# Layer change of a two-layer transformer kernel: last output round by token groups, norm factors through a diagonal, context modulated early, one modulation job on TensorE

## The chip, the cores and the metric

The kernel runs on one core of one Trainium2 chip. The metric is device time in microseconds (us), from the first to the last instruction of the program, as the median of several runs. The engines of a core run their own instruction streams in order and meet at semaphores: PE is TensorE (matmuls), DVE is VectorE, ACT is ScalarE, POOL is GpSimd, and SP issues the transfers here.

## The reference

Two layers act on 512 latent tokens and 256 context tokens of width 2048. In each layer the stream is normalised, modulated, projected, passed through four groups of attention heads with a gate, projected back, normalised, gated and added:

```python
for l in range(DEPTH):
    with_ctx = l < DEPTH - 1
    shift, scale, gate = jnp.split(silu_c @ w_mod[l] + b_mod[l], 3, axis=-1)
    shift_c, scale_c, gate_c = jnp.split(silu_cc @ w_mod[l] + b_mod[l], 3, axis=-1)
    n = rms_norm(h, pre_norm_g[l]) * (1.0 + scale[:, None]) + shift[:, None]
    nc = rms_norm(hc, pre_norm_g[l]) * (1.0 + scale_c) + shift_c
    p = jnp.split(n @ w_in[l], split_points, axis=-1)
    pc = jnp.split(nc @ w_in[l], split_points, axis=-1)
    ...
    y = (jnp.concatenate([oa, ob, on, od], axis=-1) * jax.nn.silu(p[12])) @ w_out[l]
    h = h + gate[:, None] * rms_norm(y, post_norm_g[l])
    if with_ctx:
        yc = (jnp.concatenate([oa_c, ob_c, on_c, od_c], axis=-1) * jax.nn.silu(pc[12])) @ w_out[l]
        hc = hc + gate_c * rms_norm(yc, post_norm_g[l])
return h
```

Everything is fp32. The next layer needs rms_norm(h), so its norm factor (one number for each token) is known only when all 2048 columns of a token's h are.

## The kernel before

Weights and activations are split into a high and a low part, and every fp32 product is three matmuls on the parts (`mm3`, L301 to L303; `split`, L292 on ACT for the high part, L293 on DVE for the low one). Weight tiles stream in as `wr`, become `wh` and `wl`, and stand in a pool; activations stand split in a large tile called `arena`.

A layer begins with the input projection. Its first column blocks are computed in pairs by seven products of sums of operands in place of eight (`START` and `ORDER` give the order of the products; for the first pair of a layer 1, 2, 6, 5, 7, 3, 4). A product is a *slot* of 8 k steps. The operands are token halves: `token_half` transposes one k of one half of the tokens on PE (L557), applies scale and shift on ACT (L559: one activation for latent tokens from PSUM, one for context tokens that it has loaded), and `reloads` splits the operands into the arena. `token_sums` forms sums of them for the later products. `token_n` (transposes at L548) does the other eight k later, within layer 1's stream.

A layer ends with `out_phase`. The output projection runs in rounds: one round is one block of 512 columns for four tiles of 128 latent tokens, 16 k by 12 matmuls. `evac` takes a round's result from PSUM (L1414 ACT with the sum of squares, L1415 DVE with the gate). After the last round `tail` forms the root (`rstd_of`, a chain of 9 or so small DVE instructions, L514 to L531), adds the residual (L1437, DVE; POOL at L1435 in places for the last layer), squares h on ACT for the next norm (L1443), forms the second root and scales h by it (L1452 ACT, L1454 DVE, the tile is `z`). The last round holds back its last `gs` k: it does them for tiles 0 and 1 first, then for 2 and 3, so that the first two tiles' evacuation runs beside the others' matmuls; gs is 2 in layer 0, 4 in layer 1.

While layer 0's rounds run, the next layer's modulation vectors are computed as side steps: each `mod_steps` job streams a block of `w_mod` through three `mraw` buffers and accumulates it on DVE (L441, L443), folds the halves, and sums over partitions on PE (L474). Queue orders follow the order in which the program writes its steps and a scheduler's placement of the side steps among the slots (`drive`). Layer 1's first weight tiles are prepared in the same stretch (L166 to L179, L293).

Of the kernel before, what the change touches and what calls it, by code (L numbers as in the profile page):

```python
# [47 lines left out]
RAWS = 6  # L48

# [33 lines left out]
class Kernel:  # L83
# [104 lines left out]
    def split_one(self, kind, g, key):  # L188
        if not self.need(g, 0):
            return False  # L190
        raw = g[0]
        if kind == "og":
            l, s, k = key
            hi, lo = self.og[s, k] = self.og_tiles(s, k)
        else:
            hi, lo = self.new_pair()
        self.split(hi, lo, raw)
        self.retire(g, 0)
        return True

    def load_one(self):
        nc, a = self.nc, self.a
        if self.live >= self.raws or self.wload >= len(self.lq):
            return False
        g, i, (kind, key) = self.lq[self.wload]
        if kind == "og" and key not in self.stored:
            return False
        raw = self.wp.tile([P, 512], F32, tag="wr", bufs=RAWS, name="wr")
        if kind == "in":
            l, b, c = key  # L210
            nc.sync.dma_start(raw, a["w_in"][l, b, :, 4 * c:4 * c + 4, :].rearrange("p k c -> p (k c)"))
        elif kind == "out":
            l, k, c = key
            nc.sync.dma_start(raw, a["w_out"][l, k * P:(k + 1) * P, c * 512:(c + 1) * 512])
        else:
            l, s, k = key
            w0, w = ((0, SEQ), (SEQ, CTX))[s]
            raw = raw[:, 0:w]
            nc.sync.dma_start(raw, self.ogd[l, k, :, w0:w0 + w])
        g[i] = raw  # L220
        self.live += 1
        self.wload += 1
        return True
# [81 lines left out]
    def run(self):  # L305
        tc, nc, a = self.tc, self.nc, self.a
        with ExitStack() as es:
# [41 lines left out]
            self.cnd = self.dp.tile([KT, P, CTX], F32, name="cnd")  # L349
            self.arena = base.tile([P, 7 * 8 * HT], F32R, name="arena")  # L350
# [6 lines left out]
    def plan(self):  # L357
# [8 lines left out]
        for l in range(DEPTH):  # L366
# [7 lines left out]
            for s in ((1, 0) if l < DEPTH - 1 else (0,)):  # L374
                for r in range(2 if s else 4):
                    for k in self.order:
                        if r == 0 and k != self.order[-1]:
                            self.push_one("og", (l, s, k))
                        for c in ((2 * r, 2 * r + 1) if s else (r,)):
                            self.push_one("out", (l, k, c))  # L380
# [161 lines left out]

    def token_n(self, l, k, tiles, n, t):
# [3 lines left out]
        for i, ht in enumerate(tiles):  # L547
            nc.tensor.transpose(t[:, i * P:(i + 1) * P], ht[:, k * P:(k + 1) * P], self.ident)  # L548
# [3 lines left out]
    def token_half(self, l, k, tiles, h, n, t):  # L552

        nc = self.nc
        nc.sync.dma_start(n[:, 2 * P:HT], self.cnd[k, :, h * P:(h + 1) * P])
        for i in range(2):
            nc.tensor.transpose(t[:, i * P:(i + 1) * P], tiles[2 * h + i][:, k * P:(k + 1) * P], self.ident)  # L557
        for s, view, src in ((0, n[:, 0:2 * P], t[:, 0:2 * P]), (1, n[:, 2 * P:HT], n[:, 2 * P:HT])):
            nc.scalar.activation(view, src, AF.Identity, scale=self.mA[:, l, s, k:k + 1], bias=self.mB[:, l, s, k:k + 1])  # L559
# [152 lines left out]

    def next_layer(self, l, tiles, tail):

        op = self.op


        rows = [op.tile([P, D], F32, tag="h", bufs=4, name="n") for _ in range(2)]
        ns = [[rows[k // 5][:, k % 5 * HT:(k % 5 + 1) * HT]] for k in range(8)]
        first = [lambda k=k: self.token_half(l, k, tiles, 0, ns[k][0], self.bank(1 + k % 2)) for k in range(8)]  # L720
        for a, b in zip_longest(tail, [None] * 8 + first):
# [3 lines left out]
        more = [op.tile([P, D], F32, tag="h", bufs=4, name="n") for _ in range(2)]  # L725
        for k in range(8):
            ns[k].append(more[k // 5][:, k % 5 * HT:(k % 5 + 1) * HT])
        ts = [t[:, o * HT:(o + 1) * HT] for t in (rows[1], more[1]) for o in (3, 4)]
        ts += [op.tile([P, 512], F32, tag="gp", bufs=3, name="tt")[:, 0:HT] for _ in range(3)]
        ts.append(op.tile([P, HT], F32, tag="tt", name="tt"))  # L730
        ts = [ts[2 * j:2 * j + 2] for j in range(4)]
# [4 lines left out]
        self.first = self.reloads(ns, ts)  # L736
        self.ns2 = []

        def begin():
            t = [op.tile([P, D], F32, tag="h", bufs=4, name="n") for _ in range(4)]  # L740
# [610 lines left out]
    def out_phase(self, l):  # L1351
# [3 lines left out]
        gs = 4 if last else 2  # L1355
# [3 lines left out]
        def round_slots(s, ntok, cs, done=None, early=False):  # L1359
# [18 lines left out]
            def finish(c, n0, done):  # L1378
# [3 lines left out]
                for tiles in ((0, 1), (2, 3)):  # L1382
# [8 lines left out]
            slots = [lambda n=n, c=c: slot(n, c) for n in range(KT if done is None else KT - gs) for c in cs]  # L1391
            if done is not None:
                slots.append(lambda: finish(cs[0], KT - gs, done))
# [23 lines left out]
        def tail(s, tiles, bufs, xeng):  # L1417
# [37 lines left out]

            steps = [start] + [lambda i=i, c=c: resid(i, c) for i in tiles for c in range(4)]
            if not last:
# [16 lines left out]
        if not last:  # L1474
# [6 lines left out]
            mods = self.mod_steps([(l + 1, k, c, (0, 1)) for c in range(3) for k in (1, 0)])  # L1481
# [6 lines left out]
        def xeng(i, c):  # L1488
            return nc.scalar if i % 2 else nc.vector

        for r in rounds:
            def done(tiles):
                evac(tiles, (3,), *state["acc"], state["bufs"])
                todo = tail(0, tiles, state["bufs"], xeng)
# [31 lines left out]
        self.next_layer(l + 1, state["bufs"][0], steps)  # L1526
# [81 lines left out]
```

## Time and profile before

| | us |
|---|---|
| median of 3 runs | 2696.28 (2694.01 to 2699.97) |
| profiled execution | 2691.34, its span 2689.5 |
| PE busy / DVE busy / ACT busy | 2583.6 / 2136.9 / 1285.6 |
| layer change, end of the last round to the first pair of blocks done | 1516.7 to 1583.3 |
| PE busy in it | 32.2 of 66.6 |
| last matmul of the program, last add, end of span | 2671.3, 2685.05, 2689.5 |

Times in rows of a profile are microseconds from the start of the span. A row of the timeline has the start, the duration, the engine, the line of the kernel, the tiles written and read, and in brackets how long the engine had stood idle and what released it. A row with xN groups N instructions that follow one another. A row of windows has busy time of PE, its weight loads, DVE, ACT and POOL, each with its number of instructions, then the granted clock of PE, the share of the DMA engines, and GB/s.

### The profile page before, as it was taken

What the parts mean: (1) busy time and instruction counts of PE and PEld (TensorE: products, weight loads), DVE (VectorE), ACT (ScalarE), POOL (GpSimd) and SP (SyncE); (2) the same over time, 40 slices, a digit from 0 to 9 for tenths busy, and PEclk for the clock granted to TensorE, in tenths of its full rate; (3) what the DMA queues carried; (4) which work ended last, traced back from release to release, by engine and by line L of the source; (5) the groups of instructions that cost most, each with busy time, mean ns of one, the idle gap of its engine ahead of it and who ended that gap; (6) DMA issues with size and microseconds to landing.
All of it is one profiled execution on the core that took longest, in us unless ns stands there. A gap on an engine that the chain in (4) does not pass through costs nothing. (4 is left out here: it accounts for less than half of the span.)

```text
span 2689.5 us, 41459 instructions
## 1 busy us (share of the span) xinstructions
PE 2583.6 (96%) x14392; PEld 2230.1 (83%) x14392; DVE 2136.9 (79%) x4408; ACT 1285.6 (48%) x2532; POOL 44.1 (2%) x42
## 2 busy tenths in 40 slices
PE   7899999999999999999999689999999999999997
PEld 1699999988888888887777479999978888888885
DVE  3899998678889888766889989787688887776524
ACT  3534343455556455546533464444455554544422
POOL 0000000000000000000010000000000000000001
PEclk9999999999999999999999889999999999999998
DMA  9455554422333444426886535443533434453622
GB/s 310 146 193 193 196 191 157 159 91 88 96 112 120 132 134 148 142 89 220 299 274 217 204 129 172 144 148 136 170 97 95 131 126 152 154 162 122 226 98 98
DMA packets 240994, 421.59 MB, mean 157 GB/s; under 512 B 27360, under 2 KB 68624, under 8 KB 240272
## 3 DMA queue, kind: packets, MB, share of 16 engines
q1 hardware_dynamic: 230288, 408.45, 45.9%
q10 hardware_dynamic: 10496, 10.49, 1.7%
q8 instruction: 113, 1.85, 0.3%
q14 instruction: 97, 0.79, 0.1%
HBM read 348.17 MB, written 60.19 MB: 152 GB/s over the span
## 5 line engine op out<-in xcount | busy, mean ns | idle before, releaser
L301 PE MATMUL ps<-arena,wh 128*128 128x384 f32 (+2 forms) x3104 | 1049.1, 338 | 16.6 <-ACT arena L292 7.4
L302 PE MATMUL ps<-arena,wh 128*128 128x384 f32 (+2 forms) x3104 | 1037.3, 334 | 0.2
L303 PE MATMUL ps<-arena,wl 128*128 128x384 f32 (+2 forms) x3104 | 1035.9, 334 | 0.0
L292 ACT ACTIVATE wh<-wr 128x512 fp32r<-128x512 f32 x696 | 437.6, 630 | 673.7 <-PE ps L302 349.2
L301 PEld LDWEIGHTS ps<-arena,wh 128*128 128x128 f32 x3104 | 585.7, 189 | 47.1 <-ACT arena L292 8.6
L293 DVE TENSOR_TENSOR wl<-wr,wh 128x512 fp32r<-128x512 f32 x696 | 478.4, 690 | 178.6 <-ACT wh L292 169.5
L303 PEld LDWEIGHTS ps<-arena,wl 128*128 128x128 f32 x3104 | 585.7, 189 | 32.9
L302 PEld LDWEIGHTS ps<-arena,wh 128*128 128x128 f32 x3104 | 586.5, 189 | 28.1 <-DVE arena L293 1.4
L443 DVE SCALAR_TENSOR_TENSOR macc<-mraw,sc,macc 128x512 f32<-128x512 f32 x540 | 392.5, 754 | 38.6 <-DMA mraw<-in_w_mod 37.5
L302 PE MATMUL ps<-wl,arena 128*128 128x512 f32 x640 | 256.0, 400 | 8.8 <-DVE wl L293 8.6
L303 PE MATMUL ps<-wh,arena 128*128 128x512 f32 x640 | 253.9, 397 | 0.0
L301 PE MATMUL ps<-wh,arena 128*128 128x512 f32 x640 | 248.5, 398 | 0.0
L292 ACT ACTIVATE PTh<-ps 128x512 fp32r<-128x512 f32 (+2 forms) x224 | 113.8, 518 | 114.2 <-PE ps L1127 109.0
L293 DVE TENSOR_TENSOR PTl<-ps,PTh 128x512 fp32r<-128x512 f32 (+2 forms) x224 | 130.6, 592 | 36.9 <-ACT PTh L292 35.2
L302 PEld LDWEIGHTS ps<-wl,arena 128*128 128x128 f32 x640 | 120.9, 189 | 43.4 <-DVE wl L293 16.1
L303 PEld LDWEIGHTS ps<-wh,arena 128*128 128x128 f32 x640 | 120.8, 189 | 28.5
L301 PEld LDWEIGHTS ps<-wh,arena 128*128 128x128 f32 x640 | 120.5, 189 | 27.9 <-DVE c L819 0.2
L292 ACT ACTIVATE wh<-s 128x512 fp32r<-128x512 f32 x112 | 70.8, 633 | 134.2 <-PE ps L302 94.6
L1127 PE MATMUL ps<-ident,P 128*128 128x128 f32 x672 | 112.0, 274 | 2.8 <-DVE PTl L293 1.6
L784 DVE TENSOR_TENSOR c<-ps,s 128x384 f32<-128x384 f32 (+1 forms) x168 | 87.1, 518 | 31.8 <-PE ps L303 23.4
L1127 PEld LDWEIGHTS ps<-ident,P 128*128 128x128 f32 x672 | 84.7, 140 | 31.0 <-ACT P L1106 4.7
L1083 DVE TENSOR_REDUCE small<-ps 128x1 f32<-128x768 f32 (+3 forms) x120 | 89.0, 741 | 12.2 <-PE ps L303 8.8
(261 smaller groups left out, 3146.7 us busy)
## 6 DMA issues: line engine op xcount, KB each, us to landing
wr<-in_w_in SPq DMA_DIRECT2D x448, 256.0 KB, 3.2
mraw<-in_w_mod SPq DMA_DIRECT2D x320, 256.0 KB, 3.1
wr<-in_w_out SPq DMA_DIRECT2D x192, 256.0 KB, 3.4
part<-c SPq DMA_DIRECT2D x80, 384.0 KB, 2.9
c<-part SPq DMA_DIRECT2D x80, 384.0 KB, 3.8
mr<-in_w_mod SPq DMA_DIRECT2D x32, 512.0 KB, 7.0
part<-c SPq DMA_DIRECT2D x32, 256.0 KB, 3.0
c<-part SPq DMA_DIRECT2D x32, 256.0 KB, 4.0
```

The source lines that it names most:

```text
L292: nc.scalar.activation(hi, src, AF.Copy)
L293: nc.vector.tensor_sub(lo, src, hi.bitcast(F32))
L301: mm(out, lh, rh, start=start, stop=False, skip_group_check=parts)
L302: mm(out, lh, rl, start=False, stop=False, skip_group_check=parts)
L303: return mm(out, ll, rh, start=False, stop=stop, skip_group_check=parts)
L443: nc.vector.scalar_tensor_tensor(acc, raw, col, acc, op0=ALU.mult, op1=ALU.add)
L784: self.anchors[0] = V.tensor_add(c, ps, c if m in (7, 4) else r["s"])
L1083: nc.vector.reduce_max(nm, sv, axis=AX, negate=True)
L1127: nc.tensor.transpose(T[:, i * P:(i + 1) * P], st["P", t][:, c:c + P], self.ident)
```

## The change

1. The last round holds back 9 k instead of 2 or 4 (`GS`). The groups are tiles (0, 1) and (2, 3) in layer 0, and (0, 1), (2), (3) in layer 1. Five of the nine weight pairs are kept in a free part of the arena.
2. h is not scaled by the norm factor any more for latent tokens. `turned` writes a 128 x 128 diagonal of the factors for each tile, and the transposes become products with it (`scaled`): in `token_half`, 32 of them, and `token_n`, 32.
3. `context_m` loads each of eight k of the context, modulates it on ACT and stores it, as side steps of the rounds. `token_half` loads the finished values and has one activation less.
4. One modulation job (layer 1, the third block of the shift) leaves DVE: `mod_rows` does it in 16 fp32 matmuls on PE, five written ahead of the layer change's other steps, eleven among the later ones. In PE's order one of them stands inside the last round.
5. Operands 1 and 2 are reloaded into the arena between the steps of `tail`, which run with the first half of the tokens from the start.

Line numbers move: L1415 becomes L1464, L1426 (sum for the root) L1475, L1437 L1486, L1446 (sum for the second root) L1495, L293 L297, L301 to L303 L305 to L307. New are L1509 (the diagonal), L558 (product with it), L745 (modulation on PE), L552 to L554 (context).

On DVE at the end of the last round, before (`s`, `wr` and `wl` are layer 1's weights being prepared, `sq` the squares of h):

```order
L293 TENSOR_TENSOR wl<-wr,wh 128x512
L514 TENSOR_TENSOR small<-rs 128x2
L293 TENSOR_TENSOR wl<-s_15859,wh 128x512
L515 SCALAR_TENSOR_TENSOR small<-small 128x2
L179 TENSOR_TENSOR wr<-wr,s_15859 128x512
L516 SCALAR_TENSOR_TENSOR rs<-small,rs 128x2
L293 TENSOR_TENSOR wl<-s_15858,wh 128x512
L1437 SCALAR_TENSOR_TENSOR h<-z,rs,h 128x512 x8
L166 TENSOR_TENSOR s_16014<-wr 128x512
L167 TENSOR_TENSOR s_16015<-s_16014,wr 128x512
L1446 TENSOR_REDUCE s_15647<-sq 128x2
```

and now, first at the end of group (0, 1):

```order
L521 SCALAR_TENSOR_TENSOR rs<-small,rs 128x2
L519 TENSOR_TENSOR small<-rs 128x2
L520 SCALAR_TENSOR_TENSOR small<-small 128x2
L521 SCALAR_TENSOR_TENSOR rs<-small,rs 128x2
L1486 SCALAR_TENSOR_TENSOR h<-z,rs,h 128x512 x8
L297 TENSOR_TENSOR wl<-wr,wh 128x512
L1495 TENSOR_REDUCE s_15559<-sq 128x2
L536 TENSOR_SCALAR small<-s_15559 128x2
```

then where the first diagonals and the adds of tiles 2 and 3 stand:

```order
L1509 TENSOR_SCALAR dg<-ident,r_15560 128x128 x2
L520 SCALAR_TENSOR_TENSOR small<-small 128x2
L521 SCALAR_TENSOR_TENSOR rs<-small,rs 128x2
L519 TENSOR_TENSOR small<-rs 128x2
L520 SCALAR_TENSOR_TENSOR small<-small 128x2
L521 SCALAR_TENSOR_TENSOR rs<-small,rs 128x2
L519 TENSOR_TENSOR small<-rs 128x2
L520 SCALAR_TENSOR_TENSOR small<-small 128x2
L521 SCALAR_TENSOR_TENSOR rs<-small,rs 128x2
L1486 SCALAR_TENSOR_TENSOR h<-z,rs,h 128x512 x4
L297 TENSOR_TENSOR arena<-n,arena 128x384
L1486 SCALAR_TENSOR_TENSOR h<-z,rs,h 128x512 x4
```

The residual adds of tiles 0 and 1 now follow their root chain without weight preparation in front, and the adds of tiles 2 and 3 stand between the splits of operand 1.

On PE behind the last round's last matmul, before:

```order
L302 MATMUL ps<-wl,arena 128x512
L303 MATMUL ps<-wh,arena 128x512
L474 MATMUL ps<-halves,fold 128x2 x4
L557 MATMUL ps<-ident,z 128x128 x20
L301 MATMUL ps<-arena,wh 128x384
L302 MATMUL ps<-arena,wh 128x384
L303 MATMUL ps<-arena,wl 128x384
```

and now (`mraw` and `sc` are the modulation's weights and vectors, `dg` the diagonal):

```order
L307 MATMUL ps<-wh,arena 128x512
L745 MATMUL ps<-mraw,sc 2x512 x3
L558 MATMUL ps<-dg,h 128x128 x2
L745 MATMUL ps<-mraw,sc 2x512
L558 MATMUL ps<-dg,h 128x128 x4
L305 MATMUL ps<-arena,wh 128x384
L745 MATMUL ps<-mraw,sc 2x512
L558 MATMUL ps<-dg,h 128x128 x2
L745 MATMUL ps<-mraw,sc 2x512
L558 MATMUL ps<-dg,h 128x128 x2
L306 MATMUL ps<-arena,wh 128x384
```

The fold of the last modulation job is gone from there, and matmuls of the moved job, diagonal products and the first slot's matmuls alternate.

On SP in the first of the latent rounds, before (`wr` is a weight of the projection, `h` a tile of the residual):

```order
L426 DMA mraw<-in_w_mod 128x512
L1405 DMA h<-in_x 128x512
L214 DMA wr<-in_w_out 128x512
L426 DMA mraw<-in_w_mod 128x512 x3
L214 DMA wr<-in_w_out 128x512 x2
L426 DMA mraw<-in_w_mod 128x512 x3
L214 DMA wr<-in_w_out 128x512
```

and now (`cn` is a context k, `cnd` and `cnm` its stored forms):

```order
L431 DMA mraw<-in_w_mod 128x512
L218 DMA wr<-in_w_out 128x512
L554 DMA cnm<-cn 128x256
L431 DMA mraw<-in_w_mod 128x512
L552 DMA cn<-cnd 128x256
L431 DMA mraw<-in_w_mod 128x512
L218 DMA wr<-in_w_out 128x512
L552 DMA cn<-cnd 128x256
L431 DMA mraw<-in_w_mod 128x512
L554 DMA cnm<-cn 128x256
```

The rows at L552 and L554 are new; each store at L554 waits for ACT, with loads of `mraw` and `wr` behind it.

The diff, with the parts cut that rename or only pass arguments on:

```diff
+GS = 9
@@
         if kind == "og":
             l, s, k = key
             hi, lo = self.og[s, k] = self.og_tiles(s, k)
+        elif kind == "out" and key[2:] == (3, 0) and 0 <= self.order.index(key[1]) - (KT - GS) < GS - 4:
+            o = KT * 1024 + (self.order.index(key[1]) - (KT - GS)) * 1024
+            hi, lo = self.ws[self.wsplit] = self.arena[:, o:o + 512], self.arena[:, o + 512:o + 1024]
         else:
             hi, lo = self.new_pair()
         self.split(hi, lo, raw)
...
@@
         nc.scalar.activation(cn, t, AF.Copy)
         nc.sync.dma_start(self.cnd[k], cn)
+    def context_m(self, l, k):
+
+        nc = self.nc
+        cn = self.op.tile([P, CTX], F32, tag="cn", bufs=3, name="cn")
+        nc.sync.dma_start(cn, self.cnd[k])
+        nc.scalar.activation(cn, cn, AF.Identity, scale=self.mA[:, l, 1, k:k + 1], bias=self.mB[:, l, 1, k:k + 1])
+        nc.sync.dma_start(self.cnm[k], cn)
+
+    def scaled(self, out, h, k, dg):
+
+        self.nc.tensor.matmul(out, h[:, k * P:(k + 1) * P], dg, start=True, stop=True)
+
     def token_n(self, l, k, tiles, n, t):
         nc = self.nc
         nc.sync.dma_start(ctx_of(n), self.cnd[k].rearrange("p (h t) -> p h t", h=2))
-        for i, ht in enumerate(tiles):
-            nc.tensor.transpose(t[:, i * P:(i + 1) * P], ht[:, k * P:(k + 1) * P], self.ident)
+        for i, (ht, dg) in enumerate(tiles):
+            self.scaled(t[:, i * P:(i + 1) * P], ht, k, dg)
         for s, view, src in ((0, lat_of(n), fit(t, n)), (1, ctx_of(n), ctx_of(n))):
             nc.scalar.activation(view, src, AF.Identity, scale=self.mA[:, l, s, k:k + 1], bias=self.mB[:, l, s, k:k + 1])
     def token_half(self, l, k, tiles, h, n, t):
         nc = self.nc
-        nc.sync.dma_start(n[:, 2 * P:HT], self.cnd[k, :, h * P:(h + 1) * P])
+        nc.sync.dma_start(n[:, 2 * P:HT], self.cnm[k, :, h * P:(h + 1) * P])
         for i in range(2):
-            nc.tensor.transpose(t[:, i * P:(i + 1) * P], tiles[2 * h + i][:, k * P:(k + 1) * P], self.ident)
-        for s, view, src in ((0, n[:, 0:2 * P], t[:, 0:2 * P]), (1, n[:, 2 * P:HT], n[:, 2 * P:HT])):
-            nc.scalar.activation(view, src, AF.Identity, scale=self.mA[:, l, s, k:k + 1], bias=self.mB[:, l, s, k:k + 1])
+            self.scaled(t[:, i * P:(i + 1) * P], tiles[2 * h + i][0], k, tiles[2 * h + i][1])
+        nc.scalar.activation(n[:, 0:2 * P], t[:, 0:2 * P], AF.Identity, scale=self.mA[:, l, 0, k:k + 1], bias=self.mB[:, l, 0, k:k + 1])
     def token_sums(self, ns, ts, what):
@@
         late += [lambda k=k: modulate(k) for k in range(8, KT)]
         self.late = late + self.mod_steps([(1, 1, 3, (0, 1))])
+    def mod_rows(self, l, c4, kind, bank):
+
+        nc, a = self.nc, self.a
+        ps, raws = self.bank(bank), {}
+
+        def load(k):
+            if k < KT:
+                raws[k] = self.mp.tile([P, 512], F32, tag="mraw", bufs=3, name="mraw")
+                col0 = kind * D + c4 * 512
+                nc.sync.dma_start(raws[k], a["w_mod"][l, k * P:(k + 1) * P, col0:col0 + 512])
+
+        def step(k):
+            if k == 0:
+                load(0)
+                load(1)
+            load(k + 2)
+            nc.tensor.matmul(ps[0:2], self.sc[:, k, :], raws.pop(k), start=k == 0, stop=k == KT - 1)
+
+        def columns():
+            row = self.mp.tile([P, 512], F32, tag="mraw", bufs=3, name="row")[0:2]
+            nc.scalar.activation(row, ps[0:2], AF.Copy)
+            for j in range(4):
+                nc.tensor.transpose(ps[:, 2 * j:2 * j + 2], row[:, j * P:(j + 1) * P], self.ident[0:2, 0:2])
+            self.mod_columns(l, kind, c4, ps[:, 0:8].rearrange("p (j s) -> p j s", s=2))
+
+        return [lambda k=k: step(k) for k in range(KT)] + [columns]
+
     def next_layer(self, l, tiles, tail):
         op = self.op
-
-
-        rows = [op.tile([P, D], F32, tag="h", bufs=4, name="n") for _ in range(2)]
+        fill = self.mod_rows(l, 2, 0, 6)
+        for fn in fill[:5]:
+            fn()
+
+
+        rows = [op.tile([P, D], F32, tag="z", bufs=4, name="n") for _ in range(2)]
         ns = [[rows[k // 5][:, k % 5 * HT:(k % 5 + 1) * HT]] for k in range(8)]
+        ts = []
+        self.first = self.reloads(ns, ts)
         first = [lambda k=k: self.token_half(l, k, tiles, 0, ns[k][0], self.bank(1 + k % 2)) for k in range(8)]
-        for a, b in zip_longest(tail, [None] * 8 + first):
+        first = first[:4] + self.first[1] + first[4:] + self.first[2]
+        self.first[1], self.first[2] = [], []
+        for a, b in zip_longest(tail, first):
             for fn in (a, b):
                 if fn is not None:
                     fn()
...
         self.rest = []
         for j in range(4):
             self.rest += [lambda k=k: self.token_half(l, k, tiles, 1, ns[k][1], self.bank((7, 3)[k // 4])) for k in (j, 4 + j)]
             self.rest.append(self.token_sums(ns, ts, 1)[j])
-        self.first = self.reloads(ns, ts)
+        self.rest += fill[5:]
...
@@
...
-                for tiles in ((0, 1), (2, 3)):
+                for tiles in ((0, 1), (2,), (3,)) if last else ((0, 1), (2, 3)):
                     for n, (wh, wl) in zip(range(n0, KT), ws):
                         gh, gl = self.og[s, self.order[n]]
                         for i in tiles:
@@
                     done(tiles)
                 self.look = 2
-            slots = [lambda n=n, c=c: slot(n, c) for n in range(KT if done is None else KT - gs) for c in cs]
+            slots = [lambda n=n, c=c: slot(n, c) for n in range(KT if done is None else KT - GS) for c in cs]
             if done is not None:
-                slots.append(lambda: finish(cs[0], KT - gs, done))
+                slots.append(lambda: finish(cs[0], KT - GS, done))
             return slots, accs, gps
         def open_pass(s, ntok):
@@
                 else:
                     xeng(i, c).tensor_scalar(zs[i][:, cs], hs[i][:, cs], r["r2"][:, i - t0:i - t0 + 1], 1.0, op0=ALU.mult, op1=ALU.mult)
+            def turned():
+
+                for i in tiles:
+                    dg = state["dg"][:, i * P:(i + 1) * P]
+                    nc.vector.tensor_scalar(dg, self.ident, r["r2"][:, i - t0:i - t0 + 1], None, op0=ALU.mult)
+
             steps = [start] + [lambda i=i, c=c: resid(i, c) for i in tiles for c in range(4)]
-            if not last:
+            if not last and s == 0:
+                steps += [second, turned]
+            elif not last:
                 steps += [second] + [lambda i=i, c=c: xhat(i, c) for c in range(4) for i in tiles]
             return steps
@@
-            mods = self.mod_steps([(l + 1, k, c, (0, 1)) for c in range(3) for k in (1, 0)])
+            mods = self.mod_steps([(l + 1, k, c, (0, 1)) for c in range(2) for k in (1, 0)] + [(l + 1, 1, 2, (0, 1))])
+            mods += nop * 4 + [lambda k=k: self.context_m(l + 1, k) for k in range(8)]
             bufs = None
...
-        def xeng(i, c):
-            return nc.scalar if i % 2 else nc.vector
-
         for r in rounds:
             def done(tiles):
+                if not last and tiles[0] == 0:
+                    state["dg"] = self.mp.tile([P, 512], F32, tag="mt", bufs=2, name="dg")
                 evac(tiles, (3,), *state["acc"], state["bufs"])
-                todo = tail(0, tiles, state["bufs"], xeng)
+                todo = tail(0, tiles, state["bufs"], None)
                 if last or tiles[-1] < NT - 1:
                     for fn in todo:
                         fn()
@@
         self.drive(slots[0][-1:])
         self.drive(slots[1] + slots[2] + slots[3], state["loads"], mods[n:])
         self.flush()
-        self.next_layer(l + 1, state["bufs"][0], steps)
+        self.next_layer(l + 1, [(h, state["dg"][:, i * P:(i + 1) * P]) for i, h in enumerate(state["bufs"][1])], steps)
```

More of the change, by code (lines that the diff above doesn't have):

```diff
@@ L212, in load_one @@
         elif kind == "out":
-            l, k, c = key
+            l, k, c, _ = key
             nc.sync.dma_start(raw, a["w_out"][l, k * P:(k + 1) * P, c * 512:(c + 1) * 512])
@@ L349, in run @@
             self.cnd = self.dp.tile([KT, P, CTX], F32, name="cnd")
+            self.cnm = self.dp.tile([8, P, CTX], F32, name="cnm")
             self.arena = base.tile([P, 7 * 8 * HT], F32R, name="arena")
@@ L379, in plan @@
                         for c in ((2 * r, 2 * r + 1) if s else (r,)):
-                            self.push_one("out", (l, k, c))
+                            self.push_one("out", (l, k, c, s))
     def mod_columns(self, l, kind, c4, ps):
@@ L724, in next_layer @@
                     fn()
-        more = [op.tile([P, D], F32, tag="h", bufs=4, name="n") for _ in range(2)]
+        more = [op.tile([P, D], F32, tag="z", bufs=4, name="n") for _ in range(2)]
         for k in range(8):
             ns[k].append(more[k // 5][:, k % 5 * HT:(k % 5 + 1) * HT])
[L728 to L731, printed above, removed]
+        tt = [t[:, o * HT:(o + 1) * HT] for t in (rows[1], more[1]) for o in (3, 4)]
+        tt += [op.tile([P, 512], F32, tag="gp", bufs=3, name="tt")[:, 0:HT] for _ in range(3)]
+        tt.append(op.tile([P, HT], F32, tag="tt", name="tt"))
+        ts += [tt[2 * j:2 * j + 2] for j in range(4)]
         self.rest = []
@@ L735, in next_layer @@
             self.rest.append(self.token_sums(ns, ts, 1)[j])
-        self.first = self.reloads(ns, ts)
+        self.rest += fill[5:]
         self.ns2 = []
         def begin():
-            t = [op.tile([P, D], F32, tag="h", bufs=4, name="n") for _ in range(4)]
+            t = [op.tile([P, D], F32, tag="z", bufs=4, name="n") for _ in range(4)]
             self.ns2 += [t[i // 2][:, (i % 2) * 2 * HT:(i % 2 + 1) * 2 * HT].rearrange("p (h t) -> p h t", h=2) for i in range(8)]
@@ L1354, in out_phase @@
         last = l == DEPTH - 1
-        gs = 4 if last else 2
         abanks = [0, 1, 2, 6, 7, 3, 4, 5]
```

## The prediction

> **What bounds the kernel now.** I read the page first. The tensor engine is busy for nearly the whole span, so a gain has to come from a place where it stands still, and a loss from work added where it does not.
>
> ```profile
> PE 2583.6 (96%) x14392; PEld 2230.1 (83%) x14392; DVE 2136.9 (79%) x4408; ACT 1285.6 (48%) x2532; POOL 44.1 (2%) x42
> PE   7899999999999999999999689999999999999997
> ```
>
> Then busy time by stretches: rounds 1 to 3 of layer 0's output phase (1360.00 to 1516.70), the layer change, the later stretch of token_n.
>
> ```profile
> 1360.00:1516.70 156.70, 152.46 (x672) 120.98 (x670) 147.51 (x245) 50.39 (x98) 0.00 (x0) 1.00 0.76 246
> 1516.70:1583.30 66.60, 32.20 (x132) 25.49 (x132) 54.97 (x145) 49.58 (x118) 0.00 (x0) 0.67 0.31 109
> 1816.00:1886.00 70.00, 70.00 (x500) 69.87 (x499) 53.38 (x91) 33.99 (x58) 0.00 (x0) 1.00 0.39 136
> 1417.70:1467.60 49.90, 47.61 (x209) 37.55 (x208) 49.25 (x83) 15.27 (x29) 0.00 (x0) 1.00 0.68 222
> ```
>
> At the layer change PE idles 66.6 - 32.2 = 34.4 us, at a mean clock of 0.67. In the rounds PE and DVE are both nearly full, and in round 2 (last row) DVE is full. In the stretch of token_n PE is full. So the change can win at the layer change and the kernel's end, and pays in the rounds and in token_n.
>
> The layer change on PE, from the timeline. Call S the end of the last round's last matmul: 1516.33 + 0.40 = 1516.7 before.
>
> ```profile
> 1514.70 0.40 PE L302 MATMUL ps<-wl,arena 128*128 128x512 f32 x1
> ...
> 1516.33 0.39 PE L303 MATMUL ps<-wh,arena 128*128 128x512 f32 x1
> 1517.54 1.05 PE L474 MATMUL ps<-halves,fold 128*128 128x2 f32 x8 [0.81 <-DVE fold L469]
> 1534.24 1.19 PE L557 MATMUL ps<-ident,z 128*128 128x128 f32 x4 [15.65 <-DVE z L1454]
> 1551.17 0.69 PE L301 MATMUL ps<-arena,wh 128*128 128x384 f32 x1 [3.00 <-ACT arena L292]
> ```
>
> The first transpose starts at S+17.5, the first product of layer 1 at S+34.5. The chain that leads there, on DVE (and one row of ACT):
>
> ```profile
> 1521.40 0.69 DVE L293 TENSOR_TENSOR wl<-wr,wh 128x512 fp32r<-128x512 f32 x1
> 1524.01 5.40 DVE L1437 SCALAR_TENSOR_TENSOR h<-z,rs,h 128x512 f32<-128x512 f32 x8
> 1530.65 0.15 DVE L1446 TENSOR_REDUCE s<-sq 128x2 f32<-128x8 f32 x1
> 1533.69 1.68 DVE L1454 TENSOR_SCALAR z<-h,r 128x512 f32<-128x512 f32 x4
> 1535.87 5.39 DVE L1437 SCALAR_TENSOR_TENSOR h<-z,rs,h 128x512 f32<-128x512 f32 x8
> 1542.18 0.16 DVE L1446 TENSOR_REDUCE s<-sq 128x2 f32<-128x8 f32 x1 [0.92 <-ACT z L1443]
> 1544.75 1.67 DVE L1454 TENSOR_SCALAR z<-h,r 128x512 f32<-128x512 f32 x4
> 1556.08 0.56 ACT L559 ACTIVATE n<-ps,mB,mA 128x256 f32<-128x256 f32 x1
> 1557.36 1.26 ACT L559 ACTIVATE n<-n,mB,mA 128x128 f32<-128x128 f32 x3
> 1582.72 0.56 DVE L784 TENSOR_TENSOR c<-ps,c 128x384 f32<-128x384 f32 x1
> ```
>
> The reader is to see three things. The residual add of tiles 0 and 1 starts at S+7.3, behind layer 1's weight preparation. A square-root chain takes 1544.75 - 1542.18 = 2.57 us. The second half of the tokens starts at 1556.08 = S+39.4 and the first pair of column blocks is done with the last c add, 1583.28 = S+66.6; that half takes 27.2 us.
>
> **The change part by part.**
>
> *Last round by token groups.* A matmul of 512 columns follows the next after 0.233 us (seven from 1514.70 to 1516.33, and 24 in 5.6). With 9 of 16 k held back, the first group's end T0 lies 9 x 2 x 3 = 54 matmuls, 12.6 us, ahead of S. How a group's tail runs when DVE is free is seen at the kernel's end, where group (0, 1) ends with 24 matmuls to go:
>
> ```profile
> 2670.92 0.40 PE L303 MATMUL ps<-wh,arena 128*128 128x512 f32 x1
> 2667.08 0.15 DVE L1426 TENSOR_REDUCE s<-ss 128x2 f32<-128x8 f32 x1
> 2669.64 4.77 DVE L1437 SCALAR_TENSOR_TENSOR h<-z,rs,h 128x512 f32<-128x512 f32 x4
> 2678.98 6.07 DVE L1437 SCALAR_TENSOR_TENSOR h<-z,rs,h 128x512 f32<-128x512 f32 x6
> 2670.44 6.31 POOL L1435 TENSOR_TENSOR h<-h,z 128x512 f32<-128x512 f32 x4 [201.09 <-ACT z L1434]
> ```
>
> E, PE's end, is 2671.3; group (0, 1) ended at 2671.3 - 5.6 = 2665.7; the reduce came 1.4 us later, the adds 2.56 us after that. So in the changed kernel the residual adds of tiles 0 and 1 start at T0+4 and take 5.4 (1524.01's row): done at S-3.2. Squares follow on ACT within 1.3 us (end of 1524.01's row to 1530.65 in the trace): S-1.9. The second root chain would end at S+0.7 alone, but in DVE's new order it is woven into the evacuation of tiles 2 and 3, which waits for S, and four weight splits of 0.6: the diagonals of tiles 0 and 1 come at about S+4.4, between S+1 and S+5. The 16 scalings at L1452 and L1454 go; a diagonal is a quarter of such a tile.
>
> Then the residual adds of tiles 2 and 3 stand ahead, and between, of the arena splits of operand 1: S+6 to S+12. The first product starts at about S+9 instead of S+34.5, but its eight k come only as fast as DVE splits them, until S+17, and slot 2 until S+21.5, where the diagonals of tiles 2 and 3 come. The second half starts there, not at S+39.4. It takes the 27.2 us of before less 8 context activations on ACT of 0.39 (1557.36's row, three in 1.26 with the last one's tail): 24. So the first pair is done at S+45.5 instead of S+66.6: **-21 us**. Ends: if DVE's weaving holds nothing back, S+41 (-25); if the second half stretches by the fill chain below, S+52 (-15).
>
> *The modulation job on PE.* It takes 32 products off DVE and gives PE 16 fp32 matmuls of 512 columns. Their price, from the prologue:
>
> ```profile
> 53.79 5.25 PE L650 MATMUL ps<-mr,sc 128*2 128x512 f32 x8
> 61.01 19.04 PE L650 MATMUL ps<-mr,sc 128*2 128x512 f32 x44
> mraw<-in_w_mod SPq DMA_DIRECT2D x320, 256.0 KB, 3.1
> mr<-in_w_mod SPq DMA_DIRECT2D x32, 512.0 KB, 7.0
> part<-c SPq DMA_DIRECT2D x80, 384.0 KB, 2.9
> ```
>
> Two records make one call: 19.04 / 22 = 0.87 us, up to 5.25 / 4 = 1.3 cold. One stands in round 3 ahead of S (+0.9). The next ones fill S to S+2.6 while PE would wait. Those of k 8 to 15 go through three buffers, each refilled after the matmul three earlier: about 3.1 us a hop, and end near S+34.6; the row copy, transposes and DVE's addition near S+36 are ahead of the last slots' need. They cost nothing because the second half's DVE work covers them. On DVE the 32 leave round 3 and after S.
>
> *The rounds before S.* The modulation products are spread again: in DVE's order 8 more stand ahead of round 2's end and 40 fewer in round 3.
>
> ```profile
> PE ps L302 <- DVE wl L293: 4.1, 7, 1.3
> DVE macc L443 <- DMA mraw<-in_w_mod: 7.2, 10, 1.1
> 1466.49 2.73 DVE L443 SCALAR_TENSOR_TENSOR macc<-mraw,sc,macc 128x512 f32<-128x512 f32 x4
> 1469.14 0.69 DVE L293 TENSOR_TENSOR wl<-wr,wh 128x512 fp32r<-128x512 f32 x1
> ```
>
> At (1469.14 - 1466.49) / 4 = 0.66 us each (2.73 with the last one's tail), 8 are 5.3 us of an engine that is full in round 2, and PE already waits for DVE's splits. Context's 8 round trips put eight loads and eight stores on SP's queue, between the mraw loads: each store waits for ACT, and the loads behind it with it. From nothing to half a us each: 0 to +4, I take 2. Round 3's first slots find their splits behind four evacuations and six leftover products: +2 more stall than now; its own old stall of 0.9 goes. With the matmul's 0.9 that is 5.3 + 2 + 2 - 0.9 + 0.9 = 9.3. I take off 2.3, a third of DVE's 7.2 us of waits for mraw, since a DVE that comes later waits less: **+7**, between 0 (DVE's idle hides it) and +14.
>
> *Diagonal matmuls.* In layer 1's token_n 32 transposes become products.
>
> ```profile
> 1819.33 0.60 PE L548 MATMUL ps<-ident,z 128*128 128x128 f32 x4
> 1819.68 0.36 PE L301 MATMUL ps<-arena,wh 128*128 128x256 f32 x1
> ```
>
> Four transposes hold PE for 1819.68 - 1819.33 = 0.35 us, 0.09 each. A true fp32 call costs 0.87 at 512 columns, so 0.22 at 128. PE is full there: 32 x 0.13 = **+4**; between 0 and +7 (if small ones don't scale). The 32 at the layer change lie in waits. [...]
>
> *The clock.* Before, the first product of layer 1 took 0.69 us (1551.17's row) and the stretch ran at 0.67. [...]
>
> *The kernel's end.* Three groups: (0, 1) ends at E-12.6, (2) at E-6.3, (3) at E. Before, the last add ended at 2685.05 = E+13.7. Now: adds of (0, 1) done by E-4 (4 x 1.19, the price beside POOL); tile 2 reduced at E-3, chain 2.56, three adds to E+3; tile 3 reduced at E+3.8, chain to E+6.4, three adds of 1.0 to E+9.5. **-4**, between -2 and -6.
>
> **Sum.** -21 + 7 + 4 - 4 = -14. The profiled run took 2691.34 us (span 2689.5), 4.9 below the median of the runs, 2696.28. On its scale the result is 2677, on the runs' 2682.3.
>
> **Rivals.**
>
> *A: the rounds are free.* DVE loses 32 products in all and waits 7.2 us for mraw now; if that slack takes the eight products and the stores hide, the rounds cost 0 to +2: -21 + 1 + 4 - 4 = -20, 2676. Against it: the row of round 2, 49.25 of 49.90.
>
> *B: the fill chain gates the layer change.* Loads of the last fills stand behind others in SP's queue, and PE, in order, waits at each fill with slot 6's products behind. At the 7.0 us of the mr row instead of 3.1 three hops add 12: the transition wins 9, the sum is -2, 2694. For it: three buffers only. Against it: DMA has a 0.31 share there.
>
> *C: the context round trips hold the queue (the other side).* Each is load (3.1 as mraw), ACT, store (2.9 as part): some 6.6 us with 0.5 on ACT, and mraw loads queue behind. Three buffers cover about 2 us of DVE work; if each trip beyond that stalls DVE, 8 x 4.6 = +37, with the sum -14 - 2 + 37 = +21, 2717. It makes the kernel slower from 8 x 2 us on. Against it: loads and stores are mostly several rows apart in the order.
>
> *D: the change does nothing at the layer change* because DVE's order there makes the same chain: the second half would start at S+39 again. Then +7: 2703. The order speaks against it.
>
> **How the numbers follow.** Mine 0.55 (2672 to 2690), A 0.20, B 0.14, C 0.06, D 0.05. What a measurement of this kernel can tell is about 0.2%, 5.4 us: faster means below 2690.9. Mine and A lie below but for an edge of 0.02 (0.73); B, that edge and a fifth of D within (0.17); C and the rest of D above (0.10). The range reaches down to A with the layer change at -25 and the kernel's end at -6, 2670, and a little of token_n's lower end, 2668; up to B with two more us in the rounds, 2696.
>
> **What would show it.** The first product of layer 1 at S+9 and the last c add of the first pair at S+45; residual adds of tiles 0 and 1 ending ahead of S; PE waiting for DVE's wl in the rounds for 9 to 12 us, not 4.1; token_n's stretch longer by 4; the last add at E+9.5. I am wrong if PE waits for mraw between slots 2 and 7, if DVE waits for mraw grow past 15 us in the rounds, or if the first diagonals come later than S+8.

## The result, and the profile after

The changed kernel takes 2678.84 us, the median of four runs (2676.9 to 2682.54), against 2695.61 us before in the same comparison: 16.8 us less. The ratio is 0.994, 95% interval 0.9925 to 0.9955. The forecast was 2682 us (2668 to 2696), 14 us less than before.

The profiled run is the slowest of the four, 2682.54 us (span 2680.8), and the profiled run of before lies below all four of its timed runs there, so the two traces differ by only 8.7 us. They are used for the lengths of stretches. Where these start scatters by itself: in the changed kernel and three runs below that have its order of steps up to the last round, the evacuation of round 0 comes anywhere from 1365.7 to 1371.8. The page of the changed kernel, engines and PE by slices:

```profile
PE 2601.7 (97%) x14484; PEld 2236.0 (83%) x14484; DVE 2115.0 (79%) x4383; ACT 1276.6 (48%) x2515; POOL 44.0 (2%) x42
PE   7899999999999999999999999999999999999997
```

The hollow slice at the layer change (6 and 8 tenths before) is filled. Busy time by stretches, the changed kernel: rounds 1 to 3 (from round 0's evacuation to the end S of the last round), the layer change (S to the end of the first pair's last c add), and from there to the 136th add behind it, which holds token_n.

```profile
1371.78:1528.15 156.37, 147.74 (x615) 113.94 (x614) 130.08 (x226) 54.00 (x112) 0.00 (x0) 0.97 0.70 228
1528.15:1573.53 45.38, 40.38 (x189) 24.71 (x190) 41.38 (x111) 33.24 (x78) 0.00 (x0) 1.00 0.63 203
1573.53:1901.26 327.73, 327.54 (x2342) 327.10 (x2342) 272.41 (x476) 151.31 (x272) 0.00 (x0) 1.00 0.46 154
```

The first and the third stretch of the kernel before, between the same events:

```profile
1370.10:1516.72 146.62, 142.38 (x617) 112.49 (x615) 139.40 (x230) 46.15 (x88) 0.00 (x0) 1.00 0.75 243
1583.28:1907.11 323.83, 323.64 (x2310) 323.08 (x2310) 272.22 (x478) 151.08 (x272) 0.00 (x0) 1.00 0.46 156
```

| stretch | before | after | difference | forecast |
|---|---|---|---|---|
| rounds 1 to 3 | 146.6 | 156.4 | +9.8 | +7 |
| layer change | 66.6 | 45.4 | -21.2 | -21 |
| to the 136th add (token_n) | 323.8 | 327.7 | +3.9 | +4 |
| last matmul to last add | 13.7 | 9.4 | -4.3 | -4 |

The four add up to -11.8. What else makes the 8.7 us, +1.7 ahead of round 0's evacuation and +1.4 in layer 1 behind token_n, lies outside these stretches. Where the medians' 16.8 us and the traces' 8.7 part, no trace shows: there is only one of the kernel before.

The layer change on PE: the last matmul of the last round, the fills, the first diagonal products, the first product of layer 1.

```profile
1527.75 0.40 PE L307 MATMUL ps<-wh,arena 128*128 128x512 f32 x1
1528.08 2.74 PE L745 MATMUL ps<-mraw,sc 128*2 128x512 f32 x6
1532.13 0.71 PE L558 MATMUL ps<-dg,h 128*128 128x128 f32 x4 [1.32 <-DVE dg L1509]
1534.64 0.42 PE L305 MATMUL ps<-arena,wh 128*128 128x384 f32 x1
```

And the chain on DVE: the residual adds of tiles 0 and 1, the sum for their second root, both pairs of diagonals, the first pair's last add; one row of ACT, the first activations of the second half of the tokens, stands among them.

```profile
1519.64 5.39 DVE L1486 SCALAR_TENSOR_TENSOR h<-z,rs,h 128x512 f32<-128x512 f32 x8
1526.25 0.16 DVE L1495 TENSOR_REDUCE s<-sq 128x2 f32<-128x8 f32 x1 [0.53 <-ACT z L1492]
1531.79 0.48 DVE L1509 TENSOR_SCALAR dg<-ident,r 128x128 f32<-128x128 f32 x2
1546.71 0.48 DVE L1509 TENSOR_SCALAR dg<-ident,r 128x128 f32<-128x128 f32 x2
1549.16 1.01 ACT L575 ACTIVATE n<-ps,mB,mA 128x256 f32<-128x256 f32 x2
1572.98 0.55 DVE L834 TENSOR_TENSOR c<-ps,c 128x384 f32<-128x384 f32 x1
```

With S = 1528.15, the residual adds end at S-3.1 (before: S+12.7), the diagonals come at S+3.6 and S+18.6, and the first product starts at S+6.5, not S+34.5. The second half of the tokens starts at 1549.16 = S+21.0, not S+39.4, and takes 24.4 us to the last add, not 27.2. At the kernel's end (E = 2666.51 + 0.40) the adds of the three groups:

```profile
2666.51 0.40 PE L307 MATMUL ps<-wh,arena 128*128 128x512 f32 x1
2658.38 4.82 DVE L1486 SCALAR_TENSOR_TENSOR h<-z,rs,h 128x512 f32<-128x512 f32 x4
2667.19 3.08 DVE L1486 SCALAR_TENSOR_TENSOR h<-z,rs,h 128x512 f32<-128x512 f32 x3
2673.28 3.08 DVE L1486 SCALAR_TENSOR_TENSOR h<-z,rs,h 128x512 f32<-128x512 f32 x3
```

In the rounds, what PE waited for between round 0's evacuation and S:

```profile
PE ps L306 <- DVE wl L297: 5.7, 6, 2.1
PE ps L745 <- DMA mraw<-in_w_mod: 2.4, 1, 2.4
PE ps L305 <- ACT cn L545: 0.4, 1, 0.4
```

That is 8.5 us, 4.4 more than before. But PE's busy time there rose too, from 142.38 to 147.74 with as many records, and the mean clock fell from 1.00 to 0.97. The row of the first fill, which stands in the last round ahead of S, then a stall of 2.08 us, the 3.41 us that hold this stall, and the 3.41 us behind them:

```profile
1486.57 1.44 PE L745 MATMUL ps<-mraw,sc 128*2 128x512 f32 x2 [2.37 <-DMA mraw<-in_w_mod]
1400.59 0.50 PE L306 MATMUL ps<-wl,arena 128*128 128x512 f32 x1 [2.08 <-DVE wl L297]
...
1398.29:1401.70 3.41, 1.33 (x6) 0.93 (x6) 3.18 (x7) 0.01 (x1) 0.00 (x0) 1.00 0.71 257
1401.70:1405.11 3.41, 3.41 (x10) 2.63 (x9) 2.22 (x4) 0.63 (x1) 0.00 (x0) 0.50 0.81 264
```

The reader is to see a stall that is paid for twice: 1.1 us after its end PE drops to half clock for 3.41 us, where matmuls follow each other at 0.43 us instead of 0.233, and loses another 1.6. Three stalls of the changed kernel did so (2.08, 2.13 and 2.37 us long); in the rounds of before none was longer than 1.25. The longest is the first fill's wait for its load. With its own time and the half clock behind it, the fill costs about 5 us here (2.37, then 1.36 until the next matmul starts, then six matmuls in 2.64 us instead of 1.4); the waits for splits and their two half-clock stretches make up the rest.

### The profile page after: what moved, and what is told of

The parts are those of the page before. It is cut to its first block, busy times and chain, and to the rows that moved or that the text cites. A ratio compares the mean times of both kernels' runs of the same rounds, so it can differ in the third digit from the quotient of the medians.

```text
span 2680.8 us, 41618 instructions
## 1 busy us (share of the span) xinstructions
PE 2601.7 (97%) x14484; PEld 2236.0 (83%) x14484; DVE 2115.0 (79%) x4383; ACT 1276.6 (48%) x2515; POOL 44.0 (2%) x42
## 5 line engine op out<-in xcount | busy, mean ns | idle before, releaser
L305 PE MATMUL ps<-arena,wh 128*128 128x384 f32 (+2 forms) x3104 | 1047.6, 338 | 9.2 <-ACT s L827 7.4
L307 PE MATMUL ps<-arena,wl 128*128 128x384 f32 (+2 forms) x3104 | 1034.6, 334 | 0.0
L296 ACT ACTIVATE wh<-wr 128x512 fp32r<-128x512 f32 x686 | 431.3, 630 | 640.3 <-PE ps L306 352.4
L305 PEld LDWEIGHTS ps<-arena,wh 128*128 128x128 f32 x3104 | 584.7, 188 | 41.4 <-ACT s L827 8.2
L307 PEld LDWEIGHTS ps<-arena,wl 128*128 128x128 f32 x3104 | 584.0, 188 | 33.9 <-issue 0.9
L297 DVE TENSOR_TENSOR wl<-wr,wh 128x512 fp32r<-128x512 f32 x686 | 469.5, 687 | 177.6 <-ACT wh L296 170.3
L448 DVE SCALAR_TENSOR_TENSOR macc<-mraw,sc,macc 128x512 f32<-128x512 f32 x510 | 370.6, 750 | 37.5 <-DMA mraw<-in_w_mod 36.7
L306 PE MATMUL ps<-wl,arena 128*128 128x512 f32 x600 | 241.6, 403 | 12.4 <-DVE wl L297 12.2
L307 PE MATMUL ps<-wh,arena 128*128 128x512 f32 x600 | 239.5, 399 | 0.0
L305 PE MATMUL ps<-wh,arena 128*128 128x512 f32 x600 | 230.7, 400 | 0.4 <-ACT cn L545 0.4
L297 DVE TENSOR_TENSOR PTl<-ps,PTh 128x512 fp32r<-128x512 f32 (+2 forms) x224 | 130.3, 590 | 37.7 <-ACT PTh L296 36.3
L306 PEld LDWEIGHTS ps<-wl,arena 128*128 128x128 f32 x600 | 114.0, 190 | 47.6 <-DVE wl L297 20.8
L307 PEld LDWEIGHTS ps<-wh,arena 128*128 128x128 f32 x600 | 114.1, 190 | 26.6
L305 PEld LDWEIGHTS ps<-wh,arena 128*128 128x128 f32 x600 | 113.5, 190 | 27.3 <-ACT cn L545 0.8
```

The lines of the kernel that those rows point to most:

```text
L296: nc.scalar.activation(hi, src, AF.Copy)
L297: nc.vector.tensor_sub(lo, src, hi.bitcast(F32))
L305: mm(out, lh, rh, start=start, stop=False, skip_group_check=parts)
L306: mm(out, lh, rl, start=False, stop=False, skip_group_check=parts)
L307: return mm(out, ll, rh, start=False, stop=stop, skip_group_check=parts)
L448: nc.vector.scalar_tensor_tensor(acc, raw, col, acc, op0=ALU.mult, op1=ALU.add)
```

## The experiments

Two questions were open: what makes the rounds longer (theory Q: DVE's products of the modulation stand in front of the weight splits; theory C: the context's trips hold SP's queue), and which part of the change makes the layer change shorter. The two rows under each run are its rounds 1 to 3 and its layer change, between the events named above. Where a run has one time only, it was timed once; the changed kernel's own four runs lie 5.6 us apart.

**Without the context steps.** `mods += nop * 12` in place of the eight `context_m` steps, and `token_half` as before.

> The changed kernel with empty steps in place of the eight context steps; token_half scales the context itself again, as before the change. DVE's order up to the last round is that of the changed kernel. Stretch 'rounds 1 to 3' (evacuation of round 0 to the end S of the last round): 146.7 us before, 156.1 in the changed kernel. If DVE's products in front of the weight splits make it longer (theory Q): 154 to 157, with the stalls of 2 us near the middle of rounds 1 and 2 still there. If the context's round trips on SP's queue do (theory C): 147 to 150, the stalls gone. From S to the last c add of the first pair (45.4 in the changed kernel, 66.6 before): 47 to 50, since ACT has eight more activations of 0.39 in each half.

```profile
1373.48:1526.14 152.66, 142.73 (x616) 111.47 (x615) 130.31 (x226) 50.62 (x104) 0.00 (x0) 1.00 0.68 220
1526.14:1575.77 49.63, 43.25 (x195) 27.18 (x196) 42.19 (x111) 39.23 (x94) 0.00 (x0) 0.97 0.58 186
```

One time, 2679.38 us. The rounds fell between the two theories, 3.7 us under the changed kernel. This alone does not decide: three runs below with the changed kernel's order in the rounds, trips included, took 152.4, 153.7 and 153.8, so 156.4 is the upper end of a spread and 152.7 is near its lower end. The layer change is 4.2 us longer, as expected: context modulated early is worth that much there.

**Products later.**

```diff
+        inner += mods[len(mods) - 9:]
+        del mods[len(mods) - 9:]
         n = len(mods) * len(slots[0]) // sum(len(x) for x in slots)
...
                     for n, (wh, wl) in zip(range(n0, KT), ws):
+                        if inner and not last:
+                            inner.pop(0)()
```

> The changed kernel with the eight context steps moved behind the last round's first held-back matmuls, so that DVE's products spread thinner over rounds 1 to 3: 46 and 46 in rounds 1 and 2 as before the change (48 and 54 in the changed kernel), 20 in round 3. Theory Q: rounds 1 to 3 in 148 to 150 us, the whole kernel 5 to 8 us faster than the changed one (ratio to the kernel before 0.991). Theory C says the same of the trips moved out of the way, so it is read together with the run without context steps. If neither is the cause (the held-back k make the rounds longer by themselves): 154 or more, and no gain.

```profile
1368.60:1514.27 145.67, 141.29 (x612) 111.55 (x610) 130.69 (x224) 54.24 (x111) 0.00 (x0) 1.00 0.76 244
1514.27:1561.27 47.00, 43.17 (x200) 27.28 (x199) 42.53 (x115) 34.03 (x78) 0.00 (x0) 0.96 0.62 202
```

2667.47 us (2666.8 to 2670.4, four runs) against 2695.5; ratio 0.9903, interval 0.9887 to 0.992. This beats both kernels, the changed one by 11.4 us by the medians, more than the 5 to 8 expected. The rounds cost nothing any more and the clock in them is 1.00. But the edit did not move the trips: on ACT the eight context steps run from 1415 to 1471 us, and from 1414 to 1472 in the changed kernel. Two other things moved. Of DVE's products, 54, 54 and 6 stand ahead of the evacuations of rounds 1, 2 and 3 in the changed kernel's trace, and 48, 46 and 20 in this one. And the first fill, which stood in the last round, now starts at 1515.0, behind S, so its wait left the rounds too.

**Two k held back in layer 0.** `gs = GS if last else 2`. With 16 slots in round 3 the products spread as before the change, and the context trips are still in the rounds.

> The changed kernel with 2 k held back in layer 0's last round, as before the change, 9 still in layer 1. If holding back 9 k is worth what the prediction gave it (the tail of tiles 0 and 1 beside matmuls, 7 k x 6 matmuls x 0.233 = 9.8 us of cover): from S to the last c add of the first pair 53 to 57 us, not 45.4. If the diagonals and the interleaved reload alone make the gain: 45 to 48. Rounds 1 to 3: 147 to 149 in both, since the products spread as before.

```profile
1372.40:1517.04 144.64, 141.48 (x618) 112.61 (x617) 125.65 (x209) 48.77 (x95) 0.00 (x0) 1.00 0.73 235
1517.04:1570.48 53.44, 45.54 (x196) 27.70 (x196) 48.29 (x131) 38.99 (x94) 0.00 (x0) 0.94 0.62 209
```

Thin products (48 and 44 ahead of the evacuations of rounds 1 and 2 here) give 145 us with the trips in the rounds, here and in the run before; dense ones give 152 to 156 with trips or without. So theory C is out, and a cost of the trips is not to be told from the scatter. Theory Q is not the whole cause: the first fill stands behind the last matmul of the last round in both thin runs and inside that round in the dense ones. Its wait and its own time come to 3.2 us in the run with the reload late (2.29 and 0.94), and to about 5 in the changed kernel with the half clock behind it, of the 6 to 10 us that the rounds got longer. No run moves the fill alone. Two runs below that have no fill at all, with 110 and 122 products ahead of round 2's evacuation (108 in the changed kernel, 98 before), took 160.2 and 172.7, so dense products alone make the rounds longer. Holding back 9 k is worth 8.1 us at the layer change and cost 8 to 12 in the rounds by packing the side steps into fewer slots: this kernel's one time, 2679.03, is the changed kernel's.

**The held-back k alone**, added to the kernel before.

> The kernel before with one part of the change alone: 9 k held back, three groups in layer 1, five weight pairs in the arena. From S to the last c add of the first pair: 66.6 before; if the cover of 9.8 us counts in full, 56 to 58; if DVE's weight preparation still stands in front of the residual adds, 62 to 66. From the last matmul to the last add of the kernel: 9.5 us as in the changed kernel (13.7 before). Rounds 1 to 3: 150 to 156, products denser than before.

```profile
1372.39:1532.56 160.17, 148.03 (x614) 116.59 (x612) 146.78 (x249) 48.43 (x99) 0.00 (x0) 0.95 0.69 224
1532.56:1591.20 58.64, 32.66 (x131) 26.32 (x131) 46.35 (x122) 45.82 (x108) 0.00 (x0) 0.68 0.32 109
```

The layer change gains 7.9 us and the kernel's end 4.2 (E to the last add: 9.5), and the rounds give back 13.6: 2696.66 us (one time), no gain.

**Scaling h again** in place of the diagonals (`steps += [second] + [... xhat ...]`, `nc.tensor.transpose`). The third row runs to the 136th add.

> The changed kernel with part 2 undone: h is scaled by the norm factor again (16 tiles, half on ACT, half on DVE) and the transposes are plain. If the diagonals pay at the layer change: from S to the last c add of the first pair 49 to 52 us (45.4 in the changed kernel), since four DVE scalings of 0.41 and four ACT ones of 0.71 stand in each tile pair's chain. If the chain hides them: 45 to 47. From there to the 136th add after it (327.7 in the changed kernel, 323.8 before): back to 323.8, since 32 products of 0.22 become transposes of 0.09 again.

```profile
1365.65:1519.33 153.68, 145.25 (x620) 113.03 (x619) 130.45 (x226) 54.24 (x112) 0.00 (x0) 0.99 0.71 232
1519.33:1570.44 51.11, 41.19 (x160) 22.97 (x161) 44.48 (x115) 38.25 (x86) 0.00 (x0) 0.90 0.55 180
1570.44:1893.86 323.42, 323.23 (x2307) 322.65 (x2306) 272.22 (x477) 151.08 (x272) 0.00 (x0) 1.00 0.46 156
```

The diagonals win 5.7 us at the layer change and lose 4.3 in token_n (327.73 - 323.42, 0.13 for each of 32 calls). The whole shows no gain from them: one time, 2677.83 us.

**The modulation job on DVE again** (`for c in range(3) for k in (1, 0)`, `fill = []`).

> The changed kernel with part 4 undone: the modulation job is on DVE again, six jobs in the rounds, no fp32 matmuls on PE. The side steps are 120 in place of 102 over the same 60 slots, so 56 and 60 products stand in rounds 1 and 2 on DVE (48 and 54 in the changed kernel). Theory Q: rounds 1 to 3 get longer than the changed kernel's 156.4, 160 to 166, though the wait of 2.4 us for a fill's load is gone. From S to the last c add of the first pair: 44 to 47 (45.4), if the fill chain on PE was covered; under 42 if it was not.

```profile
1372.43:1545.12 172.69, 150.49 (x625) 116.59 (x623) 144.88 (x251) 55.72 (x113) 0.00 (x0) 0.95 0.67 221
1545.12:1591.48 46.36, 31.63 (x159) 27.29 (x159) 42.49 (x111) 32.70 (x77) 0.00 (x0) 0.89 0.39 127
...
PE ps L306 <- DVE wl L297: 21.1, 13, 5.6
```

More than theory Q expected: 172.7 us, and 2700.36 in all (one time). PE waited 21.1 us for weight splits. The job on PE costs nothing at the layer change (46.4 without its fills, 45.4 with them), and without it the rest of the change is no faster than the kernel before (2695.21, eleven runs from 2691.49 to 2699.94).

**Reload late.** The order of `tail` and the reloads as before the change (`zip_longest(tail, [None] * 8 + first)`).

> The changed kernel with part 5 undone: operands 1 and 2 are reloaded after the first half of the tokens is done, and the tail of tiles 2 and 3 starts eight steps ahead of the tokens, as before the change. If the interleaving only reorders work that DVE does anyway: S to the last c add of the first pair 45 to 48 us (45.4). If it is what lets PE start early: 50 to 55. Rounds 1 to 3 as in the changed kernel, 155 to 157.

```profile
1368.55:1522.36 153.81, 145.41 (x620) 113.21 (x619) 129.75 (x226) 54.49 (x111) 0.00 (x0) 0.99 0.72 232
1522.36:1567.21 44.85, 40.83 (x189) 24.65 (x190) 41.60 (x111) 33.74 (x78) 0.00 (x0) 1.00 0.63 207
```

44.9 us: part 5 of the change is worth nothing that these traces show. The one time is 2674.25 us, below all four of the changed kernel.

**Thinner still**: fifteen steps inside the held-back matmuls (`mods[len(mods) - 15:]`, with the other steps done ahead of them) and `n -= 6`.

> The products spread thinner still: fifteen side steps (context steps and the last fold) inside the last round's held-back matmuls and six steps fewer in round 0, so DVE has 15, 46, 47 products in rounds 0 to 2 and 30 in round 3. Theory Q: the stall of 4.4 us in round 0 shrinks below 2 us and the half clock behind it goes, rounds 1 to 3 stay at 145 to 147, S to the first pair at 46 to 49: 2664 to 2667 us, 1 to 4 us below the run with the products late (2667.5). If DVE becomes late for the evacuation of tiles 0 and 1: S to first pair over 50, 2669 or more.

```profile
1369.52:1516.48 146.96, 141.97 (x618) 113.73 (x616) 133.42 (x228) 50.83 (x105) 0.00 (x0) 0.99 0.73 239
1516.48:1566.07 49.59, 44.11 (x201) 26.92 (x202) 45.37 (x124) 35.93 (x85) 0.00 (x0) 0.97 0.68 222
...
1427.86 0.50 PE L306 MATMUL ps<-wl,arena 128*128 128x512 f32 x1 [3.76 <-DVE wl L297]
```

A miss: 2674.61 us, ratio 0.9928 (0.9916 to 0.9941), 7.1 us more than with the products late. The wait for a split in round 0, 4.5 us in the run with the products late, shrank to 0.8, but PE's wait for POOL in that round grew from 2.1 to 5.1. Rounds 1 to 3 took 147.0 us, within what was expected, though a new stall of 3.76 us came in round 2, where the evacuation and five products stand ahead of a split. The layer change got 2.6 us longer than in the run with the products late.

**Two groups at the end**, `for tiles in ((0, 1), (2, 3))` in layer 1 too.

> The changed kernel with two groups, tiles (0, 1) and (2, 3), in layer 1's last round too; 9 k still held back. From the end E of the last matmul to the last add: 13.7 us before, 9.5 in the changed kernel. If the earlier first group alone makes the gain (the adds of tiles 0 and 1 are out of the way at E): 10 to 11, since tiles 2 and 3 need evacuation 1.4, chain 2.6, six adds of 1.0. If the split of tiles 2 and 3 matters: 11 to 12.5. All else as in the changed kernel: rounds 1 to 3 154 to 157, S to the first pair 45 to 46.

```profile
1367.97:1520.41 152.44, 142.66 (x614) 110.59 (x613) 130.45 (x226) 54.37 (x112) 0.00 (x0) 1.00 0.72 233
1520.41:1566.97 46.56, 41.68 (x189) 26.07 (x190) 41.38 (x111) 33.25 (x78) 0.00 (x0) 0.96 0.61 198
...
2659.27 0.40 PE L307 MATMUL ps<-wh,arena 128*128 128x512 f32 x1
2663.58 6.08 DVE L1486 SCALAR_TENSOR_TENSOR h<-z,rs,h 128x512 f32<-128x512 f32 x6
```

PE ended at 2659.67, the last add at 2669.66: 10.0 us, against 9.4 with three groups and 13.7 before. The earlier first group makes 3.7 of the 4.3 us. The one time is 2675.83 us. The layer change, which this edit does not touch, took 46.6 us, so differences of about 1 us there are within the scatter.

## Why the prediction was right, and where its steps were off

- *Layer change, -21:* -21.2. The steps came within 3 us: residual adds done at S-3.1 (S-3.2 forecast), diagonals S+3.6 (4.4) and S+18.6 (21.5), first product S+6.5 (9), second half of the tokens S+21.0 (21.5) and 24.4 us long (24), last add S+45.4 (45.5). This rules out rival D. What the parts give was measured by undoing one at a time, from 45.4 us: held-back k 8.1, diagonals 5.7, context early 4.2, job on PE 1.0, interleaving -0.5, the last two within the scatter of 1 us. These add up to 18.5; the 2.7 us left belong to no single part.
- *Rounds, +7:* +9.8 in this trace, +5.8 to +9.8 over the four traces with this order. The size was right, its make-up was not: terms that were too large and terms that were missing cancelled, so the +7 is right in part by luck. I had the eight products ahead of splits as stalls, and forecast 9 to 12 us of waiting for DVE's splits; it was 5.7, against 4.1 before. The first fill was counted at its matmul's 0.9; its load's wait of 2.4 us was not in the sum. Missing too was the half clock behind three of the stalls, about 1.6 us each: PE's busy time rose by 5.4 us. And the 2.3 us taken off because a later DVE would wait less for mraw did not come: these waits were 5.7 us before in the same stretch and 7.7 now.
- *Context trips, +2 of the 7, and rival C:* no run shows the 2 us; with thin products and the trips in place the rounds took 145 us, no longer than the 146.6 before, and rival C's +37 is ruled out.
- *token_n, +4:* +3.9. That is 0.12 us more for each of the 32 calls, 0.13 against the run that scales h again; the estimate was 0.13, the 0.87 us of 512 columns scaled to 0.22 at 128, less a transpose's 0.09.
- *The clock at the layer change:* it is 1.00 now (0.67 before), 0.90 with plain transposes and 0.89 without the fills. The run without the fills has the same length to 1 us, so there the clock is not what decides; the sum, too, has the first slots wait for DVE's splits.
- *Rival B (fill chain):* PE waited 0.4 us for a fill's load behind slot 2. *Rival A*, free rounds, was not so for this kernel and came true once the products were spread by hand; its 2676 us was too high for that, 2667.5 measured.
- *Kernel's end, -4:* -4.3.

## What to carry to other kernels

When a planner spreads side work by slots, a slot that swallows nine others makes all earlier ones denser: count side steps per microsecond of the engine that bounds, not per slot. Holding work back pays only if the engine that must prepare it has room before it; here the same edit alone gained nothing, and with one job taken off DVE and nine steps written inside the held-back matmuls, which spread DVE's products thinner and moved the first fill behind the last round, the whole change was worth 28 us instead of 17. An edit that is meant to move one thing can move others: look in the trace for where the steps went before reading its time. Undo the parts one by one: of five, one was worth nothing and one won 5.7 us in one place to lose 4.3 in another.

## What the runs showed of the hardware

PE's granted clock fell to half behind some of PE's stalls, and where these fell counted. In the traces of the two kernels it changes only at the edges of windows of 3.41 us that follow each other without a gap: the three half-clock stretches in the changed kernel's rounds begin at 1401.70, 1435.83 and 1487.03 us, 10 and 15 such windows apart. The drops went with how long PE stood idle inside one window. In rounds 1 to 3 half clock shows in six of the eleven traces: the changed kernel's and those of the runs with the held-back k alone, h scaled again, the job on DVE, the reload late and products thinner still. There, each of the eleven windows at full clock in which PE was idle for 1.93 us or more (of 3.41) was followed by one at half clock (2.08, 2.13 and 2.37 us in the changed kernel), and none in which it was idle for 1.71 or less; of those between, 1.78 and 1.79 (both with the held-back k alone) were, and 1.78 (h scaled again) and 1.83 (reload late) were not. In the other five the mean clock of the rounds is 1.00; the run with two groups at the end had a stall of 2.27 us in them. The fill's stall of 2.38 us in the run that scales h again is longer than the 2.08 shown above, but lies across an edge, 0.60 and 1.78 us idle, and the clock stays at 1.00:

```profile
1474.10:1477.51 3.41, 2.81 (x13) 1.92 (x11) 3.41 (x6) 1.15 (x2) 0.00 (x0) 1.00 0.31 109
1477.51:1480.92 3.41, 1.63 (x5) 0.71 (x6) 3.38 (x6) 1.25 (x2) 0.00 (x0) 1.00 0.64 201
1480.92:1484.34 3.42, 3.42 (x17) 2.75 (x16) 3.15 (x6) 1.21 (x2) 0.00 (x0) 1.00 0.77 239
```

In the changed kernel's rounds each half-clock stretch lasted one such window, 3.41 us. At the layer change, where PE also does fills and diagonal products, the same count does not part them: in the run with products thinner still, 1.37 us idle was followed by half clock and 1.77 us was not, and why is open.
